# Shifting the weight tiles by 96 bytes and moving the last strip to other PSUM banks in a two-block network kernel

## The chip, the cores and the metric

The kernel runs on one NeuronCore of a Trainium2 chip. The metric is the device time of one execution in microseconds (us). Three timed runs of the kernel before gave 1153.91, 1154.55 and 1156.99 us, so the median is 1154.55 us. The profiled execution, from which all rows below come, took 1154.29 us; its span from the first to the last instruction is 1152.5 us.

## The reference, cut to what matters

The reference is one pass of two transformer-like blocks over 256 tokens of width 1024, in fp32. Nearly all of its arithmetic is matrix products of the 256 token rows with weight matrices that are read once:

```python
# block 1
h = rmsnorm(x, norm_mix);  parts = split(h @ w_in)           # attention, delta rule, gates
x = x + (g0*(ya @ w_oa) + g1*(yb @ w_ob) + g2*(yc @ w_oc)) @ w_out
x = x + memory_cross_attention(...)                          # w_mq, w_mkv, w_mo
x = x + (silu(a) * b) @ w_down                               # a, b from conv(h @ w_up)
# block 2
x = x + 0.5 * rmsnorm(swiglu(h, ffn1_w_gate, ffn1_w_up, ffn1_w_down))
x = x + rmsnorm(concat(moba_attention, pool) @ w_out_2)
x = x + rmsnorm(memory_cross_attention_2(...))               # xa_wq, xa_wkv, xa_wo
x = x + 0.5 * rmsnorm(swiglu(h, ffn2_w_gate, ffn2_w_up, ffn2_w_down))
```

The feed-forward layers have 2816 hidden columns, so that their weights (1024 x 5632 up and 2816 x 1024 down, three times) are more than half of the weight bytes. The attentions are small: 256 tokens and 4 to 8 heads.

## The kernel before, in words

**Products.** TensorE has a fast form for fp32 operands, called fp32r in the kernel, which rounds them. To keep fp32 precision every weight and every activation is held as a rounded part (hi) and the rest (lo), and three products are added: hi times hi, hi activation times lo weight, lo activation times hi weight. `split_weight` makes the parts of a weight piece: ScalarE writes the hi part `wh` from the loaded piece `raw`, VectorE writes the lo part `wl` as `raw - wh`. A piece is 128 partitions by 1024 elements (512 KB) and comes by one DMA from the SP queue. There are 3 `raw` tiles, 4 `wh` and 4 `wl`, in rings.

**Jobs.** A `Job` is one strip of an output: a run of pieces over the contraction. Kind "a" has the weights stationary (128 columns loaded into the array) and an activation part of 256 tokens moving; kind "b" has the activation stationary and 512 columns of the weight part moving. `products` issues a piece's matmuls. A job's sums lie in PSUM banks: `pmm` (3 banks) for jobs, `pat` (5 banks) for the attention chains, norms and transposes. A job of 512 columns of kind "b" takes two banks, one for each half of the tokens.

**Order.** The whole order of instructions is written out by a planner in Python while the kernel is built. `Pace` keeps an estimate of when each engine is free and each value due; `Stream.pick` takes the first piece of a window of at most 4 split pieces that can start, and `Stream.start_of` says whether it can: the activation must be there, and if the job is not begun, its banks plus those of all jobs in `begun` and `pending` must fit into `PMM` = 3, or 2 for a piece that is not first in the window. `Kern.room`, `drop` and `take` do the like for the attention chains with lists of due times (`live`, with 5 entries for `pat`). The planner works with tile names and offsets inside a tile, never with addresses in SBUF.

**The last layer.** `result` makes the end: two jobs of kind "b" on `ffn2_w_down_2`, of 512 output columns each. The second carries `last=True`, which sets `Job.held`: its last two pieces are kept back and then issued bank by bank (`last_pieces`), so that the first half of the tokens can be finished while the second is still summed. When the first strip is done its callback `cb` loads a table into ScalarE, squares both banks on ScalarE (`square`) and multiplies both by a gain on VectorE (`gained`). The last strip is finished by `end`, which also writes the output by DMA.

**SBUF.** Pools lie one behind the other in the order in which `build` opens them, each tile rounded up to 32 bytes in a partition. Adding up the sizes, and taking the start of the activation tiles (`a4`, `g`) as 64 modulo 256, gives: the scratch tiles `s2`, `s1` also 64, the tile of ones `onesr` 128, the weight tiles `wh`, `wl` and `raw` 32. All slices that matmuls of jobs take begin at multiples of 512 bytes inside these tiles.

Of the kernel before, what the change touches and what calls it, by code (L numbers as in the profile page):

```python
# [6 lines left out]
F32 = mybir.dt.float32  # L7
# [4 lines left out]
PSUM = bass.MemoryType.PSUM  # L12

P = 128
# [8 lines left out]
WEIGHTS = 4  # L23
RAWS = 3
PMM = 3
LIMIT = {"s2": 6, "pat": 5, "s1": 3, "row": 4}


# [2 lines left out]
SLACK = 0.15  # L31
# [108 lines left out]
class Pace:  # L140
    HOP = 0.13

    def __init__(self, nc):
        self.free = {"pe": 0.0, "act": 0.0, "dve": 0.0, "pool": 0.0, "dma": 0.0}
        self.due = {}
        self.used = {}
        self.base = {}
        self.rings = {}
        self.count = 0
        self.now = 0.0  # L150
        self.cold = 2
        self.idles = []
        self.tile_before = None
        self.last = 0.0
        self.tensor = Queue(self, nc.tensor, "pe")
        self.scalar = Queue(self, nc.scalar, "act")
        self.vector = Queue(self, nc.vector, "dve")
        self.gpsimd = Queue(self, nc.gpsimd, "pool")
        self.sync = Queue(self, nc.sync, "dma")
# [138 lines left out]
class Act:  # L298


    def __init__(self, K, nk, tag):
        n4 = (nk + 3) // 4
        self.his = [K.a4(F32R, tag) for _ in range(n4)]
        self.los = [K.a4(F32R, tag) for _ in range(n4)]
        self.has_hi, self.has_lo = set(), set()
# [47 lines left out]
class Stream:  # L353
# [3 lines left out]

    def __init__(self, K):
        self.K = K
        self.pace = K.nc  # L360
        self.threads = []
# [83 lines left out]
    def start_of(self, pc):  # L445

        job = pc["job"]
        act = job.act.v
        ks = range(*pc["k"])
        if act is None or not all(k in act.has_hi for k in ks):  # L450
            return None
        if job not in self.begun:
            live = sum(len(j.ps) for j in self.begun + self.pending)
            if live + job.banks > PMM - (pc is not self.window[0]):
                return None
        return max([self.pace.ready(pc["hl"][0])] +
                   [self.pace.ready(act.hi(k)) - 0.2 * (k - ks[0]) for k in ks])
# [41 lines left out]
    def products(self, pc):  # L499


        K, job = self.K, pc["job"]
        nt = job.ncols // P if job.kind == "a" else 2
        if job.held is not None and job.left <= 2:
            job.held.append(pc)
            if len(job.held) == 2:
                self.last_pieces(job.held)
            job.left -= job.left == 2
            return
        if job.kind == "a":  # L510
            at = lambda n: job.ps[n // 2][:, n % 2, :]
        else:
            at = lambda n: job.ps[n].rearrange("p a b -> p (a b)")
        if job.ps is None:
            job.ps = [K.pmm() for _ in range(job.banks)]
            self.begun.append(job)
            first = True
        else:
            first = False
        act = job.act.v  # L520
        hi, lo = pc["hl"]
        ks = range(*pc["k"])
        known = all(k in act.has_lo for k in ks)
        early = known and max(self.pace.ready(act.lo(k)) for k in ks) <= self.pace.now + 0.8
        order = (0, 2, 1) if early else (0, 1, 2)
        for i in order:
            if i == 2:
                self.wait(lambda: all(k in act.has_lo for k in ks))
            for k in ks:
                for n in range(nt):  # L530
                    out = at(n)
                    x = act.lo(k) if i == 2 else act.hi(k)
                    if job.kind == "a":
                        s = (k - ks[0]) * job.ncols + n * P
                        a, b = (lo if i == 1 else hi)[:, s:s + P], x
                    else:
                        s = slice((k - ks[0]) * 512, (k - ks[0]) * 512 + 512)
                        a, b = x[:, n * P:n * P + P], (lo if i == 1 else hi)[:, s]
                    K.mm(out, a, b, first and k == ks[0] and i == 0 and (n % 2 == 0 or job.kind == "b"),
                         job.left == 1 and k == ks[-1] and i == order[-1])  # L540
            if i != order[-1]:
                self.step()
        job.left -= 1
        if job.left == 0:
            self.begun.remove(job)
            self.pending.append(job)
# [13 lines left out]
class Kern:  # L560
    def __init__(self, tc, pools, aps):
# [4 lines left out]
        self.n = 0  # L566
        self.live = {k: [0.0] * m for k, m in LIMIT.items()}

# [51 lines left out]
    def s1(self, tag="s1"):  # L620
        t = self.take(tag)
        w = 16 + T if tag == "row" else T
        return self.nc.begin(self.p["s1"].tile([P, w], F32, tag=tag, bufs=LIMIT[tag], name=self.nm(tag)), t)

# [1417 lines left out]
def build(tc, aps):  # L2042
    from contextlib import ExitStack
    nc = tc.nc
    with ExitStack() as es:
        pool = lambda name, bufs, **kw: es.enter_context(tc.tile_pool(name=name, bufs=bufs, **kw))
        bufs = {"x": 1, "c": 1, "a": 12, "s2": 6, "s1": 3, "tiny": 8, "sq": 4, "rb": 4, "wh": 4, "wl": 4, "raw": 3,
                "pmm": 3, "pat": 5}
        pools = {n: (pool(n, b, **({"space": PSUM} if n in ("pmm", "pat") else {})), b) for n, b in bufs.items()}
        K = Kern(tc, pools, aps)  # L2050
        c = K.p["c"]
        K.onesr = c.tile([P, P], F32R, name="onesr")
        K.vec0 = c.tile([P, NVEC0], F32, name="vec0")
        K.vec = c.tile([P, NVEC - NVEC0], F32, name="vec")
        K.con = c.tile([P, NCON], F32, name="con")
        K.poolw = c.tile([P, 4, P], F32, name="poolw")
        K.ypad = c.tile([P, 4, 260], F32, name="ypad")
        K.cf = c.tile([P, T], F32R, name="cf")
        K.cg = c.tile([P, T], F32R, name="cg")
        K.selr = c.tile([P, 8], F32R, name="selr")  # L2060
        with tc.manual_schedule():
            nc.gpsimd.memset(K.onesr.bitcast(F32), 1.0)
            nc.gpsimd.memset(K.ypad[:, :, 0:4], 0.0)
            nc.gpsimd.memset(K.cf.bitcast(F32), 0.0)
            nc.gpsimd.memset(K.cg.bitcast(F32), 0.0)
            model(K, aps)
# [104 lines left out]
```

## Time and profile before

| | |
|---|---|
| median of three timed runs | 1154.55 us |
| profiled execution | 1154.29 us |
| its span | 1152.5 us |
| PE busy | 1126.1 us (98% of the span), 9108 matmuls |
| PEld (weight loads) busy | 1074.6 us |
| DVE (VectorE) busy | 762.5 us |
| ACT (ScalarE) busy | 668.1 us |
| POOL (GpSimd) busy | 250.1 us |
| mean granted TensorE clock | 0.994 |
| DMA | 193.96 MB, mean 168 GB/s |

Matmuls overlap: one row of the trace says when a group of matmuls began, and the end of a group is modelled. The distance from the beginning of one group to the beginning of the next, divided by the number of matmuls, is therefore the spacing, and it is less than the duration that the profile prints for one matmul. Starts are printed to 0.01 us.

### The profile page before, as it was taken

What the parts mean: (1) busy time and instruction counts of PE and PEld (TensorE: products, weight loads), DVE (VectorE), ACT (ScalarE), POOL (GpSimd) and SP (SyncE); (2) the same over time, 40 slices, a digit from 0 to 9 for tenths busy, and PEclk for the clock granted to TensorE, in tenths of its full rate; (3) what the DMA queues carried; (4) which work ended last, traced back from release to release, by engine and by line L of the source; (5) the groups of instructions that cost most, each with busy time, mean ns of one, the idle gap of its engine ahead of it and who ended that gap; (6) DMA issues with size and microseconds to landing.
All of it is one profiled execution on the core that took longest, in us unless ns stands there. A gap on an engine that the chain in (4) does not pass through costs nothing.

```text
span 1152.5 us, 22341 instructions
## 1 busy us (share of the span) xinstructions
PE 1126.1 (98%) x9108; PEld 1074.6 (93%) x9108; DVE 762.5 (66%) x1015; ACT 668.1 (58%) x1085; POOL 250.1 (22%) x235
## 2 busy tenths in 40 slices
PE   8999999999999999999999999999999998999997
PEld 7998998999988999999999999999989998999976
DVE  6885785558886588998556555448876747555543
ACT  5447773465786566666545554546667557555442
POOL 0020130022141023333015333012102112533200
PEclk9999999999999999999999999999999999999999
DMA  7554533236564365556656555665444534666652
GB/s 244 180 170 152 193 111 111 93 111 199 169 200 146 101 193 183 183 183 190 203 160 218 191 190 177 201 194 160 167 148 147 152 92 140 205 192 207 196 191 91
DMA packets 56550, 193.96 MB, mean 168 GB/s; under 512 B 6400, under 2 KB 6528, under 8 KB 56448
## 3 DMA queue, kind: packets, MB, share of 16 engines
q1 hardware_dynamic: 56304, 192.54, 52.3%
q8 instruction: 71, 1.16, 0.4%
q14 instruction: 31, 0.25, 0.1%
q10 hardware_dynamic: 144, 0.01, 0.0%
HBM read 191.47 MB, written 1.05 MB: 167 GB/s over the span
## 4 chain that ended last, share of the span: by engine, by line
PE 65%; DVE 16%; ACT 7%; issue 6%; DMA 4%; POOL 1%; SPq 0%; DVEq 0%; ACTq 0%; POOLq 0%
PE pmm L291 58%; PE pat L291 8%; DVE wl L291 6%; ACT wh L291 3%; DVE s L291 3%; DVE a L291 3%; DMA raw<-w_in 3%; ACT s L291 2%; DVE g L291 1%; DMA raw<-w_up 1%; DVE sg L291 1%; DVE ypad L291 1%; POOL s L291 1%; ACT g L291 1%; ACT L291 1%
## 5 line engine op out<-in xcount | busy, mean ns | idle before, releaser
L291 DVE TENSOR_TENSOR wl<-raw,wh 128x1024 fp32r<-128x1024 f32 (+1 forms) x370 | 455.3, 1238 | 283.1 <-ACT wh L291 279.4
L291 PE MATMUL pmm<-a,wh 128*128 128x256 f32 x3856 | 505.0, 281 | 7.2 <-DVE a L291 5.2
L291 PEld LDWEIGHTS pmm<-a,wh 128*128 128x128 f32 x3856 | 474.3, 189 | 13.3 <-DVE a L291 6.9
L291 ACT ACTIVATE wh<-raw 128x1024 fp32r<-128x1024 f32 (+1 forms) x370 | 372.5, 1019 | 166.4 <-PE pmm L291 58.1
L291 PE MATMUL pmm<-a,wl 128*128 128x256 f32 x1928 | 269.8, 281 | 2.4 <-DVE wl L291 1.8
L291 PEld LDWEIGHTS pmm<-a,wl 128*128 128x128 f32 x1928 | 244.0, 188 | 5.8 <-DVE wl L291 4.4
L291 PE MATMUL pmm<-g,wh 128*128 128x256 f32 x1088 | 140.3, 280 | 0.1
L291 PEld LDWEIGHTS pmm<-g,wh 128*128 128x128 f32 x1088 | 132.6, 188 | 0.8 <-POOL g L291 0.3
L291 POOL TENSOR_TENSOR sq<-sq,sq 128x512 f32<-128x512 f32 x30 | 41.9, 1398 | 342.4 <-ACT sq L291 304.9
L291 POOL TENSOR_TENSOR s<-s 128x256 f32<-128x256 f32 x66 | 71.9, 1089 | 175.7 <-ACT s L291 169.3
L291 ACT ACTIVATE s<-s 128x256 f32<-128x256 f32 (+4 forms) x118 | 56.1, 478 | 91.2 <-DVE s L291 76.9
L291 POOL TENSOR_TENSOR g<-s,g 128x256 fp32r<-128x256 f32 x66 | 64.5, 978 | 60.0 <-ACT g L291 60.0
L291 PE MATMUL pmm<-g,wl 128*128 128x256 f32 x544 | 75.6, 280 | 0.0
L291 PEld LDWEIGHTS pmm<-g,wl 128*128 128x128 f32 x544 | 68.7, 188 | 0.1
L291 ACT ACTIVATE g<-s 128x256 fp32r<-128x256 f32 x66 | 27.3, 413 | 56.7 <-POOL s L291 56.7
L291 PE MATMUL pmm<-wh,g 128*128 128x512 f32 x208 | 55.4, 405 | 2.9 <-DVE a L291 1.9
L291 POOL TENSOR_TENSOR s<-s,s 128x512 fp32r<-128x512 f32 (+1 forms) x25 | 33.4, 1342 | 105.7 <-ACT s L291 101.0
L291 PEld LDWEIGHTS pmm<-wh,g 128*128 128x128 f32 x208 | 39.8, 193 | 13.0 <-DVE a L291 2.2
L291 DVE SCALAR_TENSOR_TENSOR s<-ypad,vec,s 128x256 f32<-128x256 f32 x88 | 45.7, 578 | 0.0
L291 PE MATMUL pmm<-wh,a 128*128 128x512 f32 x160 | 42.0, 401 | 0.0
L291 DVE TENSOR_TENSOR s<-pmm,rb 128x512 f32<-128x512 f32 x44 | 30.2, 688 | 16.1 <-PE pmm L291 16.1
L291 ACT ACTIVATE a<-x,vec 128x256 fp32r<-128x256 f32 x54 | 24.8, 501 | 21.5 <-DVE x L291 21.4
(165 smaller groups left out, 874.5 us busy)
## 6 DMA issues: line engine op xcount, KB each, us to landing
raw<-ffn_w_up SPq DMA_DIRECT2D x82, 512.0 KB, 4.2
raw<-w_in SPq DMA_DIRECT2D x78, 512.0 KB, 4.3
raw<-ffn_w_down SPq DMA_DIRECT2D x42, 512.0 KB, 4.3
raw<-w_up SPq DMA_DIRECT2D x41, 512.0 KB, 4.3
raw<-w_down SPq DMA_DIRECT2D x20, 512.0 KB, 4.3
raw<-w_out SPq DMA_DIRECT2D x16, 512.0 KB, 4.4
raw<-xa_wkv SPq DMA_DIRECT2D x16, 512.0 KB, 4.0
raw<-w_mkv SPq DMA_DIRECT2D x8, 512.0 KB, 4.1
```

The lines of the kernel that those rows point to most:

```text
L291: return fn(*args, **kwargs)
```

## The change

Two things change. In `build` a pool named `gap` with one tile of 24 fp32 elements (96 bytes in a partition) is opened just ahead of the pool `wh`; nothing reads or writes it. The pools `wh`, `wl` and `raw` behind it start 96 bytes later: `wh` and `wl` go from 32 to 128 modulo 256, where the activations stay at 64. For kind "a" the stationary operand was 32 bytes ahead of (below) the moving one modulo 256, and is 64 bytes behind (above) it.

Second, the job with `held` (the last strip) takes its two banks from `pat` and not from `pmm`: `products` calls `K.pat()` twice, and `start_of` asks for two `pat` banks that are due, and no longer counts the job among the users of `pmm`.

```diff
+GAP = 24
@@ start_of
-            live = sum(len(j.ps) for j in self.begun + self.pending)
-            if live + job.banks > PMM - (pc is not self.window[0]):
+            live = sum(len(j.ps) for j in self.begun + self.pending if j.held is None)
+            if job.held is not None:
+                if len(self.K.live["pat"]) < job.banks or sorted(self.K.live["pat"])[job.banks - 1] > self.pace.now + SLACK:
+                    return None
+            elif live + job.banks > PMM - (pc is not self.window[0]):
                 return None
@@ products
-            job.ps = [K.pmm() for _ in range(job.banks)]
+            if job.held is None:
+                job.ps = [K.pmm() for _ in range(job.banks)]
+            else:
+                job.ps = [K.pat().rearrange("p (a b) -> p a b", a=2) for _ in range(job.banks)]
@@ build
-        pools = {n: (pool(n, b, **({"space": PSUM} if n in ("pmm", "pat") else {})), b) for n, b in bufs.items()}
+        pools = {}
+        for n, b in bufs.items():
+            if n == "wh":
+                pools["gap"] = (pool("gap", 1), 1)
+            pools[n] = (pool(n, b, **({"space": PSUM} if n in ("pmm", "pat") else {})), b)
         K = Kern(tc, pools, aps)
+        K.p["gap"].tile([P, GAP], F32, name="gap")
```

## Rows read from the trace of the kernel before

**Rows 1.** The page: PE's busy time and share, and the granted clock by slices.
```profile
PE 1126.1 (98%) x9108; PEld 1074.6 (93%) x9108; DVE 762.5 (66%) x1015; ACT 668.1 (58%) x1085; POOL 250.1 (22%) x235
PEclk9999999999999999999999999999999999999999
```

**Rows 2.** PE's groups by shape: out<-in, count, busy us, mean ns, idle before.
```profile
L291 PE MATMUL pmm<-a,wh 128*128 128x256 f32 x3856 | 505.0, 281 | 7.2 <-DVE a L291 5.2 <-ACT wh L291 1.7
...
L291 PE MATMUL pmm<-g,wh 128*128 128x256 f32 x1088 | 140.3, 280 | 0.1
...
L291 PE MATMUL pmm<-wh,g 128*128 128x512 f32 x208 | 55.4, 405 | 2.9 <-DVE a L291 1.9 <-DVE sg L291 1.0
L291 PE MATMUL pmm<-wh,a 128*128 128x512 f32 x160 | 42.0, 401 | 0.0
```

**Rows 3.** PE's waits: us in total, times, longest us.
```profile
PE pmm L291 <- DVE wl L291: 1.8, 3, 0.8
...
PE pmm L291 <- ACT wh L291: 1.7, 5, 0.7
```

**Rows 4.** Timeline of PE in a feed-forward layer: start us, us, instruction, count.
```profile
649.97 2.03 PE L291 MATMUL pmm<-a,wh 128*128 128x256 f32 x16
651.84 1.10 PE L291 MATMUL pmm<-a,wl 128*128 128x256 f32 x8
652.77 0.40 PE L291 MATMUL pmm<-a,wh 128*128 128x256 f32 x2
```

**Rows 5.** Timeline of PE: fp32r matmuls of 256 columns with onesr stationary.
```profile
347.58 0.63 PE L291 MATMUL pat<-s,onesr 128*128 128x256 f32 x4
348.06 0.50 PE L291 MATMUL pat<-onesr,s 128*128 128x1 f32 x4
```

**Rows 6.** Timeline of PE: fp32r matmuls of 512 columns with onesr stationary.
```profile
113.82 0.63 PE L291 MATMUL pat<-s,onesr 128*128 128x512 f32 x2
114.29 0.64 PE L291 MATMUL pmm<-a,wh 128*128 128x256 f32 x4
```

**Rows 7.** Timeline of PE: plain fp32 passes of 256 columns, and fp32r behind them.
```profile
366.18 3.61 PE L291 MATMUL pat<-g,a 128*128 128x256 f32 x16
369.44 1.29 PE L291 MATMUL pmm<-a,wl 128*128 128x256 f32 x8
370.56 0.63 PE L291 MATMUL pmm<-a,wh 128*128 128x256 f32 x4
```

**Rows 8.** Timeline of all engines at the end of the last strip.
```profile
1142.99 1.10 PE L291 MATMUL pmm<-wh,g 128*128 128x512 f32 x4
1143.66 0.60 ACT L291 ACTIVATE sq<-pmm 128x512 f32<-128x512 f32 x1 [8.27 <-PE pmm L291]
...
1145.79 0.63 PE L291 MATMUL pmm<-wh,g 128*128 128x512 f32 x2
1146.46 0.60 ACT L291 ACTIVATE sq<-pmm 128x512 f32<-128x512 f32 x1 [1.55 <-PE pmm L291]
```

**Rows 9.** Timeline of all engines where the last strip begins.
```profile
1110.62 1.06 ACT L291 ACTIVATE wh<-raw 128x1024 fp32r<-128x1024 f32 x1 [1.74 <-PE pmm L291]
...
1111.36 2.03 PE L291 MATMUL pmm<-wh,g 128*128 128x512 f32 x8
...
1113.22 1.09 PE L291 MATMUL pmm<-wl,g 128*128 128x512 f32 x4
...
1114.16 0.39 PE L291 MATMUL pmm<-wh,g 128*128 128x512 f32 x1
...
1114.84 1.29 DVE L291 TENSOR_TENSOR sg<-pmm,a 128x512 f32<-128x512 f32 x2 [1.90 <-ACT sq L291]
...
1115.28 1.06 ACT L291 ACTIVATE wh<-raw 128x1024 fp32r<-128x1024 f32 x1
1115.59 1.90 PE L291 MATMUL pmm<-wh,g 128*128 128x512 f32 x7 [1.04 <-DVE sg L291]
```

## The prediction

> **What bounds the kernel now.** [...] The groups by shape say which matmuls [rows 2]: of kind "a" 3856 + 1088 = 4944 with `wh`, and half as many with `wl`, because hi·hi and lo·hi use `wh` and only hi·lo uses `wl`; that is 7416 of 256 columns. Of kind "b" it is 368 and 184, so 552 of 512 columns. Then the timeline gives the spacing, from start to start: in a feed-forward layer 24 matmuls take from 649.97 to 652.77, 2.80 us, so 116.7 ns each [rows 4]; in the last layer 12 matmuls of 512 columns take from 1111.36 to 1114.16, 233.3 ns each [rows 9]. 7416 x 0.1167 = 865 us and 552 x 0.2333 = 129 us: 994 of the 1152.5 us are these two streams, the rest being attention matmuls and gaps between stages. Waits for the weights' parts are small: PE stood 1.8 us for `wl` and 1.7 us for `wh` in the whole run [rows 3].
>
> Is there something in 116.7 ns that an address could give back? Sixteen passes of plain fp32 with 256 columns and the eight fp32r matmuls behind them take from 366.18 to 370.56; less 8 x 0.1167, 3.45 us are left, 215 ns a pass [rows 7]. If fp32r streamed at just twice that rate, 256 columns would take 108 ns and 512 columns 215. So 9 ns of each kind "a" matmul and 18 ns of each kind "b" one are an excess over the doubled plain rate: 7416 x 9 = 67 us and 552 x 18 = 10 us. 77 us is all that a placement of operands could be worth.
>
> **The last strip's banks.** The first strip ends, the last one's first matmul starts at 1114.16 into the third bank, and the next starts at 1115.59, released by VectorE's product on the first strip's bank [rows 9]. Without a wait it would follow after 0.23 us. 1.43 - 0.23 = 1.20 us go when the banks come from `pat`, which has five and serves only chains and norms, none of which runs in the last layer. Everything behind is one stream of matmuls until the last bank is read, so the end moves by the same 1.20 us, if no wait takes its place. What is late next: ScalarE does the first strip's table load and squares between two splits of weights, so `wh` is written at 1115.28 where the step of 2.8 us from 1110.62 would have put it at 1113.42, 1.9 us late [rows 9]. That piece goes into a ring of four whose next use is three pieces of 2.8 us after its slot came free, 8.4 us; the two parts take 1.06 us and some 1.2 us and there are over 5 us of reserve, so 1.9 + 1.2 us fit. No job but this one is planned otherwise, since `held` is None for all the rest and the order of pieces in the window stays. Price: -1.20 us; at worst 0 (the wait comes back as one for `wh`).
>
> **The gap.** It adds no instruction and no wait, and the planner knows no addresses, so the order of all instructions stays. It can only act through where operands lie. For ScalarE, VectorE and the DMA the three tiles `raw`, `wh`, `wl` move together. If a split got slower or faster, the PE would see it only through the 3.5 us of waits above [rows 3]; I take 0, bounds -3.5 and a few us.
>
> For TensorE the question is whether the load of the next weights, which runs beside each matmul, slows the moving stream, and whether that hangs on the distance of the two addresses modulo 256. The trace has the new distance already: `onesr` (128) stationary against `s2` tiles (64) moving is 64 bytes behind, what `wh` against `a` will be. Four such matmuls of 256 columns take from 347.58 to 348.06, 120 ns each, which in starts printed to 0.01 us is 117 to 123 [rows 5]; two of 512 columns take from 113.82 to 114.29, 235 ns each [rows 6]. Against 116.7 and 233.3 at the present distances (-32 for "a", +32 for "b") that is no gain, and a loss of at most 3.3 and 1.7 ns.
>
> A second test needs no address: a matmul beside which no weights load. The last strip ends bank by bank. In its first bank the final two matmuls begin at 1142.99, with the other bank's loads running beside the last of them, and ScalarE, which waits for that bank, starts at 1143.66; in its second bank they begin at 1145.79, nothing loads any more, and ScalarE starts at 1146.46 [rows 8]. Both times 0.67 us. Had the load cost the stream its 18 ns, the second would be one or two hundredths shorter. At the resolution of a hundredth the load is not what makes the 18 ns, and then no distance can bring them back.
>
> Bounds from both sides: -77 us if the whole excess goes [rows 2, 7]; above, 7416 x 3.3 ns + 552 x 1.7 ns = +25.4 us if the new distance costs what the `onesr` rows show at their most [rows 5, 6]. The two rows nearest in kind (same distance, and no load at all) both say that the spacing stays, so I take 0.
>
> [...]
>
> Sum against the profiled execution: 1154.29 - 1.20 + 0 = 1153.1 us. Its time lies 0.26 us under the median of 1154.55, so the two need no correction.
>
> **The rivals.** *The two reads do meet, and the new distance parts them.* For it: the spacing is the same 116.7 ns throughout the dense stretch, an excess which the plain fp32 passes, at half the rate, don't have. Against it: [rows 6, 8]. If a third of the excess goes, 1153.1 - 26 = 1127 us; all of it, 1076 us. A tenth, 1145.4, would be seen already.
>
> *The new distance costs.* The place is the moving stream of every kind "a" matmul, the price at the most the 3.3 ns of [rows 5]: 1153.1 + 25.4 = 1178.5 us, at half of it 1166 us. It decides from (1.2 + 3.5) us / 7416 = 0.6 ns a matmul on, which no row here can exclude. Against it: those four matmuls also change operands and bank at either end, and the 512 column pair shows just 1.7 ns.
>
> *The change doesn't do what it says at the end.* PE waits at the last strip for the late `wh` instead, and the time stays at 1154.3 us.
>
> **How the numbers follow.** The forecast, banks alone, has 0.45, and its own range is 1150 to 1156 us. The empty third rival has 0.05. The parted reads get 0.34, since 77 us of excess has a cause that I can't name from the trace, and I put two thirds of that on gains under 28 us. The cost gets 0.16, three quarters of it below half its price. Within 0.3% (3.5 us, about what a measurement of this kernel can tell from no change): 0.45 + 0.05 = 0.50; faster 0.34; slower 0.16. The range reaches down to a third of the excess, 1125, and up to half of the cost, 1166, and leaves out 0.11 and 0.04.
>
> **What would show it.** The dense stretch of the first feed-forward layer of block 2 shows 24 matmuls in 2.80 us again if the gap does nothing; 2.59 us would be the whole excess, 2.88 us the cost. The last layer's 12 matmuls show 2.80 us likewise. The last strip's second matmul follows its first after 0.23 us, and the wait for `sg` is gone from PE's waits. I am wrong if the spacing anywhere in the dense stretches moves by over 0.6 ns, or if PE waits for `wh` or `wl` in the eight microseconds after the last strip begins.

## The result and the profile after

The changed kernel takes 1143.04 us (median; 1141.01 to 1146.95) beside 1155.28 us for the kernel before: ratio 0.9897, 95% interval 0.9867 to 0.9928. The forecast of 1153.1 us was the case "banks alone, gap at nothing"; what came is the rival in which the distance between the two operands gives back a part of the excess. The profiled execution took 1142.6 us with a span of 1140.8 us, 11.7 us less than before. The order of the matmuls is the same, and the helper's line 291 is line 292 now.

The page of after, engine totals and granted clock by slices:

```profile
PE 1108.9 (97%) x9108; PEld 1058.2 (93%) x9108; DVE 762.9 (67%) x1015; ACT 668.5 (59%) x1085; POOL 252.8 (22%) x235
PEclk9899999999999999999999999999999999999999
```

PE is busy for 17.2 us less than in [rows 1] with the same 9108 matmuls, but the time in which it is not busy grew from 1152.5 - 1126.1 = 26.4 us to 31.9 us. So the matmuls became faster, and 5.5 us of that came back as waiting.

PE's groups by shape in after (out<-in, count, busy us, mean ns, idle before), which answer to [rows 2]:

```profile
L292 PE MATMUL pmm<-a,wh 128*128 128x256 f32 x3856 | 496.9, 280 | 10.4 <-DVE a L292 5.4 <-ACT wh L292 4.0 <-DVE s L292 0.7
...
L292 PE MATMUL pmm<-g,wh 128*128 128x256 f32 x1088 | 137.4, 278 | 0.4 <-DVE g L292 0.4
```

The same counts take 496.9 us for 505.0 and 137.4 for 140.3, while the idle time ahead of the first group rose from 7.2 to 10.4 us, with `wh` as a releaser for 4.0 in place of 1.7.

Two stretches of PE's timeline in after (start us, us, instruction, count). The first is the dense stretch that answers to [rows 4], the second lies in the stage of the convolution:

```profile
642.22 1.98 PE L292 MATMUL pmm<-a,wh 128*128 128x256 f32 x16
644.03 1.07 PE L292 MATMUL pmm<-a,wl 128*128 128x256 f32 x8
644.93 1.98 PE L292 MATMUL pmm<-a,wh 128*128 128x256 f32 x16
```

```profile
479.62 2.05 PE L292 MATMUL pmm<-a,wh 128*128 128x256 f32 x16
481.50 1.10 PE L292 MATMUL pmm<-a,wl 128*128 128x256 f32 x8
482.44 2.05 PE L292 MATMUL pmm<-a,wh 128*128 128x256 f32 x16
```

In the first, 24 matmuls take 2.71 us, 113 ns each (116.7 before); in the second 2.82 us, 117.5 ns. From all starts of the trace, these are two fixed spacings, 113.3 and 117.8 ns. In this trace a stretch keeps the one it has until PE next stops or changes its kind of matmul; the longest, 1487 matmuls from 602 us on, stands at 113.3 ns. Some 1200 of the kind "a" matmuls stood at 117.8, most others at 113.3. The kernel before has two spacings as well: of its settled kind "a" matmuls (those behind the first nine of a stretch) about one in eight stood at 117.8 ns, the others at 116.7. So the change moved the lower of two spacings and left the upper one where it was. The mean over the run went from 116.84 to 114.36 ns, and for kind "b" from 233.15 to 229.59.

PE's waits in after (us in total, times, longest us), beside [rows 3]:

```profile
PE pmm L292 <- ACT wh L292: 4.0, 7, 1.4
PE pat L292 <- DVE x L292: 3.1, 3, 1.9
PE pat L292 <- POOL s L292: 3.0, 4, 1.4
PE pmm L292 <- DVE wl L292: 2.9, 6, 1.1
```

The two waits for weight parts grew from 3.5 to 6.9 us. All of PE's waits together went from 18.9 to 25.3 us, although the one for `sg` at the last strip is gone.

The last layer of after on PE, its passage to the last strip (which answers to [rows 9]) and then its end ([rows 8]):

```profile
1101.63 1.99 PE L292 MATMUL pmm<-wh,g 128*128 128x512 f32 x8
1103.46 1.08 PE L292 MATMUL pmm<-wl,g 128*128 128x512 f32 x4
1104.38 1.99 PE L292 MATMUL pat<-wh,g 128*128 128x512 f32 x8
...
1134.13 0.63 PE L292 MATMUL pat<-wh,g 128*128 128x512 f32 x2
1134.79 0.60 ACT L292 ACTIVATE sq<-pat 128x512 f32<-128x512 f32 x1 [1.50 <-PE pat L292]
```

Twelve matmuls of 512 columns take 2.75 us (2.80 before). All eight of the last strip's first piece run without a stop, in `pat` banks.

### The profile page after: what moved, and what is told of

It is laid out like the page before. It is cut to its first block, busy times and chain, and to the rows that moved or that the text cites. A ratio compares the mean times of both kernels' runs of the same rounds, so it can differ in the third digit from the quotient of the medians.

```text
span 1140.8 us, 22341 instructions
## 1 busy us (share of the span) xinstructions
PE 1108.9 (97%) x9108; PEld 1058.2 (93%) x9108; DVE 762.9 (67%) x1015; ACT 668.5 (59%) x1085; POOL 252.8 (22%) x235
## 4 chain that ended last, share of the span: by engine, by line
PE 70%; DVE 12%; ACT 7%; DMA 5%; issue 4%; POOL 1%; SPq 0%; DVEq 0%; ACTq 0%; POOLq 0%
PE pmm L292 60%; PE pat L292 11%; DVE wl L292 6%; ACT wh L292 3%; DVE a L292 2%; DMA raw<-w_in 2%; DVE g L292 1%; ACT s L292 1%; DVE sg L292 1%; DMA raw<-ffn_w_up 1%; ACT L292 1%; DVE s L292 1%; ACT g L292 1%; DVE x L292 1%; DMA raw<-w_ob 1%
## 5 line engine op out<-in xcount | busy, mean ns | idle before, releaser
L292 PE MATMUL pmm<-a,wh 128*128 128x256 f32 x3856 | 496.9, 280 | 10.4 <-DVE a L292 5.4
L292 PEld LDWEIGHTS pmm<-a,wh 128*128 128x128 f32 x3856 | 466.8, 189 | 17.1 <-DVE a L292 7.2
L292 PE MATMUL pmm<-a,wl 128*128 128x256 f32 x1928 | 266.5, 280 | 3.0 <-DVE wl L292 2.9
L292 PEld LDWEIGHTS pmm<-a,wl 128*128 128x128 f32 x1928 | 240.9, 189 | 6.8 <-DVE wl L292 5.3
L292 PE MATMUL pmm<-g,wh 128*128 128x256 f32 x1088 | 137.4, 278 | 0.4 <-DVE g L292 0.4
L292 PEld LDWEIGHTS pmm<-g,wh 128*128 128x128 f32 x1088 | 130.1, 188 | 1.0 <-DVE g L292 0.6
L292 PEld LDWEIGHTS pmm<-wh,a 128*128 128x128 f32 x160 | 29.4, 188 | 6.8 <-DVE g L292 0.7
L292 DVE SCALAR_TENSOR_TENSOR a<-x,vec,a 128x256 fp32r<-128x256 f32 x56 | 32.9, 623 | 2.3 <-ACT a L292 2.3
```

What stands on the lines that cost most here:

```text
L292: return fn(*args, **kwargs)
```

## The experiments

A name like "distance 64" below means: start of the stationary operand minus start of the moving one, in bytes, modulo 256. Kind "a" goes from 224 to 64 by the change, kind "b" from 32 to 192. The streams below vary the distance from 0 to 240 bytes, so that it repeats after 256 bytes was not tested. Each of the streams alone, and each of the two kernels without taps, was executed once.

**Does the spacing hang on the distance at all?** A stream of matmuls alone, 48 to a distance.

```diff
+for d in range(16):                       # distance 16*d bytes
+    for i in range(48):
+        matmul(o, st[:, (i % 8)*128 + 4*d :][:, :128], mv[:, (i % 4)*256 :][:, :256])
+# then 512 columns, then stationary operands of 32 columns, then both starts moved
```

> A kernel of its own that leaves the network out: groups of 48 fp32r matmuls (24 of 512 columns) with nothing on the other engines, the weights' start varied against the moving start. Theory D (what counts is stationary start minus moving start modulo 256): at 224 a 256 column group has 116.7 ns a matmul, at 64 it has 113.3 ns, as in the two kernels; 512 columns at 32 have 233.3 ns and at 192 have 229.2 ns; moving both starts together changes nothing. Theory S (the weights' own start counts): the four groups with the same distance and other starts differ by 3 ns. On the cause: if the load beside makes the excess over 108 ns, loads of 32 columns in place of 128 leave about a quarter of it, so 110 ns or less at every distance; if the stream makes it by itself, they stay at 113 to 117 ns.

PE's timeline of this stream, one row for each distance: 0 and 16 (from 21.96), 64 and 80 (from 44.74), 224 and what follows (from 101.26), and loads of 32 columns at distances 64, 96 and 128 (from 168.50):

```profile
21.96 5.92 PE L37 MATMUL oc<-mv,st 128*128 128x256 f32 x48
27.72 5.85 PE L37 MATMUL od<-mv,st 128*128 128x256 f32 x48
...
44.74 5.61 PE L37 MATMUL og<-mv,st 128*128 128x256 f32 x48
50.18 5.86 PE L37 MATMUL oh<-mv,st 128*128 128x256 f32 x48
...
101.26 5.76 PE L37 MATMUL oa<-mv,st 128*128 128x256 f32 x48
106.86 5.92 PE L37 MATMUL ob<-mv,st 128*128 128x256 f32 x48
...
168.50 5.62 PE L37 MATMUL oe<-mv,st 128*32 128x256 f32 x48
173.95 5.60 PE L37 MATMUL of<-mv,st 128*32 128x256 f32 x48
179.39 5.61 PE L37 MATMUL og<-mv,st 128*32 128x256 f32 x48
```

From start to start: 5.76 us at distance 0 (120.0 ns each), 5.44 us at 64 (113.3), 5.60 us at 224 (116.7). Of sixteen distances 64 and 192 gave 113.3, the rest 116.6 to 120.1. With 512 columns, 192 gave 229 ns and 32 gave 233; distance 0 was fast there, 227. With both starts moved together, 224 stayed at 116.7, but 64 gave 113.3 twice and 117.8 twice. So the distance decides, and at 64 something more does. Loads of 32 columns came down to 113.3 ns at more distances (also at 96 and 128, where loads of 128 columns stood at 118.8 and 118.5) and never lower. So at some distances the load does slow the stream, but a quarter of the load does not bring back what is left at 113.3.

**The gap alone and the strip alone.**

```diff
 gap alone:    + pools["gap"] ahead of "wh", tile [P, 24];  start_of and products as before
 strip alone:  start_of and products as changed;  no pool "gap"
```

> The gap of 96 bytes without the last strip's other banks. If the gap makes the gain, the time is 1.20 us above the full change (ratio to before about 0.991) and the dense stretch shows 24 matmuls in 2.72 us; if the gain came from the order or the banks, the ratio is 1.00.

> The last strip in the chains' banks without the gap. By the prediction 1.20 us go and nothing else: ratio 0.999, the second matmul of the last strip 0.23 us behind the first, dense stretch 24 matmuls in 2.80 us as before.

The gap alone took 1144.65 us, ratio 0.9921 (0.9891 to 0.9952); the strip alone 1155.43 us, 0.9993 (0.9977 to 1.0009). PE's timeline of the gap alone, the dense stretch and a stretch at 551 us:

```profile
551.60 2.05 PE L291 MATMUL pmm<-g,wh 128*128 128x256 f32 x16
553.48 1.10 PE L291 MATMUL pmm<-g,wl 128*128 128x256 f32 x8
554.43 2.05 PE L291 MATMUL pmm<-g,wh 128*128 128x256 f32 x16
...
639.84 1.98 PE L291 MATMUL pmm<-a,wh 128*128 128x256 f32 x16
641.66 1.07 PE L291 MATMUL pmm<-a,wl 128*128 128x256 f32 x8
642.56 1.98 PE L291 MATMUL pmm<-a,wh 128*128 128x256 f32 x16
```

2.72 us for 24 at 640 us, but 2.83 us at 551 us, a stretch that in the profiled run of after was fast. PE's timeline of the strip alone at the passage to the last strip:

```profile
1111.27 2.03 PE L291 MATMUL pmm<-wh,g 128*128 128x512 f32 x8
1113.14 1.09 PE L291 MATMUL pmm<-wl,g 128*128 128x512 f32 x4
1114.07 2.03 PE L291 MATMUL pat<-wh,g 128*128 128x512 f32 x8
```

No stop is left there, 2.80 us for twelve as before, and the span is 1151.1 us, 1.4 us under that of before. Nearly the whole change in time is the gap's; the strip's 1.2 us are below what timing can tell.

**Is it the distance, or the place of the weights?** The gap in front of the activations moves everything behind it, the weights to 128 as in the change, but the distance stays 224.

```diff
-            if n == "wh":
+            if n == "a":
                 pools["gap"] = (pool("gap", 1), 1)
```

> The same 96 bytes, but in front of the activations: weights at 128 modulo 256 as after the change, activations at 160, so that their distance stays 32 bytes ahead as before. Theory D: spacing 116.7 ns in the dense stretch, ratio 1.00. Theory S (weights' own place, or the place of raw and wh for ScalarE, VectorE and DMA): spacing 113.3 ns, ratio 0.99.

1157.17 us, ratio 1.0011 (0.9995 to 1.0027). The mean spacing was 117.11 ns; no stretch stood at 113.3, nearly half of the settled matmuls at 117.8 and the others at 116.7. Moving the weights does not bring the gain; the distance does.

**A distance that should cost.** A gap of 32 bytes puts stationary and moving operands of kind "a" at distance 0.

```diff
-GAP = 24
+GAP = 8        # no change of the last strip's banks
```

> A gap of 32 bytes in place of 96, so that weights and activations start at the same place modulo 256 (distance 0), with the last strip as before. Theory D with the distances measured alone: 120.0 ns a kind a matmul, 7416 x 3.3 ns = 24.5 us more, and 227.4 for kind b, 552 x 5.9 ns = 3.3 us less; about 1.018 of before, slower. If any move away from 32 bytes ahead helped, it would be faster.

1167.54 us, ratio 1.0089 (1.0061 to 1.0118). PE's timeline in the dense stretch:

```profile
646.24 2.08 PE L291 MATMUL pmm<-a,wh 128*128 128x256 f32 x16
648.16 1.12 PE L291 MATMUL pmm<-a,wl 128*128 128x256 f32 x8
649.12 2.08 PE L291 MATMUL pmm<-a,wh 128*128 128x256 f32 x16
```

2.88 us for 24, 120.0 ns as in the stream alone: a theory that knows only the distance has this spacing right. Its price came to half: over the run kind "a" cost 7416 x 2.99 ns = 22.2 us more and kind "b" 552 x 5.25 ns = 2.9 us less, but the span grew by 11.4 us only. PE's waits shrank from 18.9 to 15.5 us. That table counts a wait only from the modelled end of the matmul before, which lies over 100 ns behind the next possible start (a mean of 281 ns is printed for a kind "a" matmul, where the next one starts after 116.7), and so misses part of it. From all starts, kind "a" spacings of 130 ns and more at a granted clock of 1.00 (waits and changes of operand) held 23.1 us above the run's mean in the kernel before, 14.8 here and 29.5 in after. The 8.3 us that went here account for the 7.9 us that are missing from the price. The slower PE waited less here (15.5 us by the table, beside 18.9), as the faster one of after waited more (25.3).

**Where did the gain of the change go?** In the stage of the convolution VectorE has the taps of the convolution to do beside the splits. Both kernels were run without the taps.

```diff
-        for k in (1, 0):
+        for k in ():
```

> The kernel before without the two earlier taps of the convolution in the first feed-forward layer (the output is that of a convolution of one tap), which takes four VectorE instructions of 0.58 us from each of its 22 units. For comparison with e6. If that stage waited on VectorE, it gets shorter; by the trace PE waits only 0.2 us there for split weights, so I expect under 2 us.

> The changed kernel with the same two taps left out. Theory W (what the matmuls gain in the convolution stage comes back as waits for VectorE's and ScalarE's weight splits): with the load off VectorE the stage is shorter than in e5 by what the spacing gives, 1081 matmuls x 2 to 3.4 ns = 2 to 3.7 us, where the full kernels differ by 0.4 us. If the gain is lost elsewhere (the pace itself), the difference stays near 0.4 us.

Busy time between the same two matmuls, the 3201st and the 4301st (to 0.05 us); before and after as they are, then before and after without taps. The columns are the window, its length in us, the busy us (and instructions) of PE, PEld, DVE, ACT and POOL, the granted clock, DMA's share and its GB/s:

```profile
384.71:516.16 131.45, 130.78 (x1103) 129.31 (x1102) 110.01 (x152) 83.67 (x136) 43.25 (x39) 1.00 0.56 174
```
```profile
385.54:516.59 131.05, 129.12 (x1102) 127.46 (x1101) 110.42 (x152) 83.30 (x136) 43.86 (x39) 1.00 0.56 174
```
```profile
386.18:517.49 131.31, 131.31 (x1102) 131.31 (x1101) 82.62 (x84) 87.20 (x143) 54.00 (x42) 1.00 0.57 181
```
```profile
384.04:513.34 129.30, 129.07 (x1103) 128.74 (x1101) 81.33 (x83) 86.47 (x142) 52.50 (x42) 1.00 0.57 183
```

With the taps VectorE is busy for 110 of 131 us; PE's busy time falls by 1.66 us and the stage by 0.40. PE's waits for `wh` and `wl` in it were 0.2 us before and 2.0 us after. Without the taps VectorE is busy for 82 us; PE's busy time falls by 2.24 us and the stage by 2.01.

This pair does not measure the change, though, for its streams stood elsewhere than those with taps. The first kernel without taps ran at 120.0 ns from 411 to 600 us, the second at 117.8 nearly throughout from 409 to 786 us. By all starts the mean spacing in this stage was 117.05 ns before and 115.10 after, and without taps 119.38 and 116.92. At its 119.38 ns the kernel before got only 0.14 us shorter here without its taps. The whole times of the pair, 1156.39 and 1146.80 us, are not compared for the same reason.

What the rows do show is read at like spacing: 117.05 ns with taps took 131.45 us, 116.92 ns without taps 129.30 us. And with taps the stage hardly follows the spacing. Over the eight profiled runs of the network with taps (two of them stand below) the mean in this stage lay between 114.57 and 119.97 ns, worth 5.9 us over its 1098 kind "a" matmuls, but the stage took between 130.43 and 132.32 us, and the two ends of the spacing took 131.38 and 132.32. So it is VectorE's load that holds this stage: the splits come late, and a faster stream runs into them.

**What picks 113.3 or 117.8?** Groups of 24 matmuls, the network left out, each group behind one "divider" matmul of another length.

```diff
+for d in distances:                        # 19 of them
+    for n in (60, 76, 100, 116, 140, 164, 188, 220):
+        matmul(x, st, mv[:, :n]);  24 matmuls at distance d
```

> Groups of 24 fp32r matmuls of 256 columns alone, each distance eight times, each time behind one other matmul of 60 to 220 columns, which sets the group off at another moment. If the distance decides alone (theory D as it stands), the eight groups of one distance agree. If the distance only allows a fast pace and the moment of the start picks it (theory L, a lock), the eight groups of distance 64 are some at 113.3 and some at 117.8 ns, as the changed kernel's stretches are. Period 256: 192 is as slow as 224 (116.7); period 128: 192 has groups at 113.3 like 64. Steps of 4 bytes around 64: with lines or banks of 16 bytes or more, 60 and 68 lie near 64.

At distance 64 the eight groups stood at 113.3, 113.3, 113.3, 117.8, 117.8, 117.8, 113.3, 117.8. At 60 and 68 bytes none came under 117, at 192 all eight were at 117.8, at 224 they lay between 116.4 and 117.8. So among these distances the fast spacing is 64's alone (192 can have it, and had it in the first stream), and there something ahead of a stream picks one of two. Next, 18 lengths at distance 64, eight groups of each:

```diff
-for n in (60, 76, 100, 116, 140, 164, 188, 220)   at 19 distances
+for n in (64, 76, ... 244): eight times n, at distance 64
```

> The network is left out: only groups of 24 fp32r matmuls of 256 columns at distance 64 run, each behind one matmul of n columns; 18 lengths n from 64 to 244, eight groups of each. Theory S: the length of the divider alone sets the lock, so all eight groups of one n are alike, all 113.3 ns or all 117.8, and some n always gives 113.3 (by the run before, n of 60 to 100 and 188 may). Theory H: the lock also hangs on the state that the divider found, so that a length keeps or swaps it: at some lengths the eight groups alternate between 113.3 and 117.8, and no length turns every slow group into a fast one. Theory R: neither, eight groups of one length fall without an order, about as often on 113.3 as on 117.8. Only under S could a divider in front of the dense stretches win back what is left, (114.36 - 113.33) x 7416 = 7.6 us.

PE's timeline behind dividers of 116 columns:

```profile
159.37 0.22 PE L37 MATMUL x<-mv,st 128*128 128x116 f32 x1
159.42 3.05 PE L39 MATMUL oa<-mv,st 128*128 128x256 f32 x24
162.31 0.22 PE L37 MATMUL x<-mv,st 128*128 128x116 f32 x1
162.36 2.95 PE L39 MATMUL oa<-mv,st 128*128 128x256 f32 x24
165.15 0.22 PE L37 MATMUL x<-mv,st 128*128 128x116 f32 x1
```

The two periods are 2.94 and 2.84 us, and so on in turn: slow, fast, slow, fast. The same alternation holds at 128 to 152 and 176 to 200 columns. From 64 to 108 columns, and at 164, 212, 232 and 244, all eight were fast; at 220 they went slow, slow, fast. The order repeats without chance in it, and it hangs on the length and on what the divider found, which contradicts the theory in which the length alone decides. The spacing found is not all of that, though: at 220 columns a slow group is followed once by a slow one and once by a fast one. What short dividers do to a slow group, that run did not show:

```diff
-    (n,) * 8
+    (100, 116, n, 116, n, 220, 220, n)
```

> The network is left out: again only groups of 24 fp32r matmuls of 256 columns at distance 64, each behind one matmul of n columns. In each row of eight groups the lengths are 100, 116, n, 116, n, 220, 220, n, for n from 32 to 512. The run before showed that 116 and 220 columns turn a fast group (113.3 ns) into a slow one (117.8 ns). If the lock hangs on the length and on the state found, as that run says, the second, fourth and sixth group are slow wherever the one before was fast, and the third and fifth show what n does to a slow state. Theory K: short dividers (up to 108 columns) set the fast state whatever they find: third, fifth and eighth group at 113.3 for these n. Theory H: they only keep what they find: third group at 117.8 for short n, and a row whose sum is longer by 24 x 4.4 ns = 0.11 us for each group that stays slow. Under K a divider in front of the long stretches would be worth a trial, at the 0.13 us that it takes there; under H none is.

From 32 to 92 columns a divider turned every slow group fast, and so did 212, 232 and 512; 100 did too, a little later in the group, and 108, 164 and 244, which keep a fast group fast, left a slow one slow. So in the bare stream a short divider seemed to be a cure, and it was tried in the network.

```diff
+    if job.kind == "a":
+        K.since += 1
+        if first and k == ks[0] and i == 0 and n == 0 and K.since > 300:
+            matmul(out[:, 0:64], a, b[:, 0:64], start=True, stop=False);  K.since = 0
     K.mm(out, a, b, ...)
```

> The changed kernel with 22 short matmuls more: at the beginning of a kind a job, when more than 300 kind a matmuls have gone by since the last one, its first matmul is preceded by one with the same operands cut to 64 columns, which the real one overwrites. Theory K (the runs with the network left out: 64 columns always leave the fast state behind them): each stretch that such a matmul opens runs at 113.3 ns until the next wait of PE, also those that ran at 117.8 in one or another of the runs so far (1487 matmuls from 602 us, 465 from 543 us, 911 from 971 us). Cost 22 x 0.13 = 2.9 us. Gain: in the profiled run of the changed kernel 1188 matmuls stood at 117.8, of which some 400 would lie behind such a matmul, 1.8 us; in the run of the gap alone 3.4 us; in the run without taps 13 us. So against the changed kernel -10 to +1 us, the median about 2 us lower, 1141 us, and its runs closer together. Rival: the place of the start inside the network decides otherwise than in the bare stream, the slow stretches stay, and the time is 2.9 us higher, 1146 us.

> The changed kernel as it is, on the same chip as the run with the short matmuls, so that the two can be compared: 1143 us by the first timing, 1141 to 1147 for single runs. If the two states of the stream make its scatter, its runs lie further apart than those of the kernel with the short matmuls, and one or two of its long stretches stand at 117.8 ns in one execution and at 113.3 in another.

The kernel with dividers took 1152.41 us, ratio to before 0.9968 (0.9951 to 0.9984); the changed kernel as it is 1146.93 us beside it, 0.9918 (0.9885 to 0.9950). PE's timeline with dividers, one at 647 and one at 685 us:

```profile
644.55 2.05 PE L292 MATMUL pmm<-a,wh 128*128 128x256 f32 x16
646.43 1.11 PE L292 MATMUL pmm<-a,wl 128*128 128x256 f32 x8
647.37 0.20 PE L549 MATMUL pmm<-a,wh 128*128 128x64 f32 x1
647.40 2.08 PE L292 MATMUL pmm<-a,wh 128*128 128x256 f32 x16
649.32 1.07 PE L292 MATMUL pmm<-a,wl 128*128 128x256 f32 x8
650.23 1.98 PE L292 MATMUL pmm<-a,wh 128*128 128x256 f32 x16
...
684.68 1.07 PE L292 MATMUL pmm<-a,wl 128*128 128x256 f32 x8
685.59 0.19 PE L549 MATMUL pmm<-a,wh 128*128 128x64 f32 x1
685.62 2.13 PE L292 MATMUL pmm<-a,wh 128*128 128x256 f32 x16
687.58 1.10 PE L292 MATMUL pmm<-a,wl 128*128 128x256 f32 x8
688.52 2.05 PE L292 MATMUL pmm<-a,wh 128*128 128x256 f32 x16
```

At 647 us the divider turns a slow stream fast (8 matmuls from 649.32 in 0.91 us); the next, at 685 us, turns the fast one slow (8 from 684.68 in 0.91 us, 8 from 687.58 in 0.94). Of the 22 dividers sixteen stood behind 24 or more settled matmuls without a break. All ten that met a fast stream left it slow; of the six that met a slow one three left it slow and three turned it fast. In the profiled executions (1153.49 us and 1141.31) the mean spacing was 115.87 ns with dividers and 114.48 without. So the theory of the cure is wrong in the network. There the divider shares its stationary operand and its bank with the matmul behind it and lies at distance 64, where in the stream alone it lay at 0; which of these matters was not tried. The rival had the spacing's failure right, but not its size: it expected 1146 us, since it let the slow stretches stay and did not foresee that fast ones would turn slow.

The second run of the changed kernel shows its scatter: single runs lay from 1141.3 to 1153.8 us, where 1147 was expected as the longest, and further apart than the kernel's with dividers (1150.8 to 1158.9), as was expected. By its median the gain is 9.8 us, by that of the first run 12.2. The profiled execution of the second run had 305 matmuls from 280.5 us at 117.8 ns, of which 250 had run at 113.3 in that of the first. Whether such stretches make the scatter is not shown, since the long runs left no trace.

## Why the prediction was right or wrong, step by step

The time of 1143.0 us lies between the 1125 and 1166 of the prediction, but in the share of a rival: the forecast's own range, 1150 to 1156, missed it. That the wide range holds it comes from the rivals' shares and not from the mechanism that was forecast.

*What bounds the kernel.* Right in the main: the two streams of matmuls are 994 of the 1152.5 us, and the time moved when their spacings moved. It did not move by as much, because the stage of the convolution is held by its splits (VectorE busy for 110 of 131 us). And a 9 in the row of the clock [rows 1] stands for 90% or more, not for the whole clock: from 28.8 to 57.6 us of the kernel before the granted clock was 0.94.

*The last strip's banks, -1.20 us.* Right. The wait for `sg` is gone, no wait for the late `wh` took its place, and the strip alone shortened the span by 1.4 us.

*The gap at nothing.* This step failed: "the two rows nearest in kind [...] both say that the spacing stays, so I take 0". The gain is 116.84 - 114.36 = 2.48 ns for each of 7416 kind "a" matmuls, 18.4 us, and 233.15 - 229.59 = 3.56 ns for each of 552 of kind "b", 2.0 us. The line of 0.6 ns, at which I said I would be wrong, is passed fourfold. Both pieces of evidence were too weak for what was put on them:

- [rows 5, 6] are four and two matmuls at a change of operands. The runs show that the spacing belongs to a stream that has settled: behind a stop even fast stretches begin with slower ones (their first nine average 114 to 116 ns). A settled stream at distance 64 has 113.3 or 117.8 ns, and the 120 ns of [rows 5] are neither.
- [rows 8] have a resolution of 10 ns, and the effect on one matmul of 512 columns is 4 ns. The end of after shows 0.66 us where before showed 0.67. The step from "the load does not make the 18 ns" to "no distance can bring them back" was no inference either. The runs agree with the first half only for the floor (a quarter of the load stays at 113.3 ns; at distances 96 and 128 it took 5 ns off), and they contradict the second.

That the place of one operand beside the other counts for this kind of matmul is what the streams alone show: with the same shapes and the same two operand tiles their spacing was 120.0, 116.7 and 113.3 ns at distances 0, 224 and 64.

*The excess of 77 us as the lower bound.* It held, but was far too wide. The spacing never fell under 113.3 ns, at any distance or size of load that was tried, so no placement that was tried came to the 108 ns of the doubled plain rate. 116.7 - 113.3 = 3.4 ns, 25 us in all, was what one could give kind "a", and 7416 x 2.48 ns is three quarters of it. The quarter that is missing is mostly the stretches at 117.8.

*Splits and waits.* I looked only for splits that become slower. What happened is that PE became faster and met the splits as they were. The account of the profiled run: spacings -18.4 and -2.0, last strip -1.2, together -21.6 us. Of this came back 7.4 us as waits of PE (18.9 to 25.3 us, apart from the 1.0 for `sg` that the strip took away), and about 2.1 us because 21 more matmuls of kind "a" had spacings over 200 ns instead of 117. Where the granted clock was 0.50 and not 1.00 (in before from 29.9 to 33.3 us, for one), kind "a" stood at 213 to 214 ns; after has 37 such spacings and before 24 (the mean granted clock was 0.88 from 28.5 to 57 us and 0.98 from 100 to 200 us of after, beside 0.94 and 1.00 in before). The strip alone has as many spacings over 200 ns, so they need not be the gap's work. That makes -12.1 us; the span shows -11.7. The waits' part is shown for the stage of the convolution by the runs with and without taps; for the other stages before 580 us it is read from the table of waits alone.

*The rivals.* "The two reads do meet" came true in its result, a part of the excess given back by the new distance; that it is the two reads which meet is not shown. Of its three prices the smallest, a tenth of the excess with 1145.4 us, was the nearest to 1143.0. "The new distance costs" is not true of the change: its slower spacing, 117.8 ns, occurs at the old distance too, and the 120.0 ns that would have been this rival's price came at distance 0, not at 64.

## What to carry to other kernels

In this kernel, which is bound by long streams of equal matmuls, 2.48 and 3.56 ns of spacing were nearly the whole gain, and they were not to be read from short groups or from two-digit durations: a bare stream of 48 matmuls for each placement showed in one run that a placement can be faster (113.3 ns at 64 beside 116.7 at 224), though not which of its spacings a stream in the kernel will take. Take the gain of a faster stream stage by stage, as the smaller of what the stream gives and what its suppliers have in reserve; here 9.9 of 21.6 us did not arrive, 7.4 of them because PE waited more. And before a stage is compared over two runs, compare the spacings at which they stood. A cure that works in the bare stream is still to be tried in the kernel, with the operands and banks that it has there: here the mean spacing was 115.87 ns with it and 114.48 without.

## What the runs showed of the hardware

- For fp32r matmuls of 256 columns the spacing hung on the distance of stationary and moving operand: in this case's streams alone (m1_offsets, m2_modes) it was 120.0 ns at 0, 116.7 at 224, 113.3 or 117.8 at 64, and never under 117 at 60 and 68 bytes. With 512 columns it was 227 at 0, 233 at 32 and at 64, 229 at 192 (m1_offsets).
- At distance 64 the stream had two spacings, 113.3 and 117.8 ns, and the faster was kept for 1487 matmuls (after, from 602 us). A single matmul between groups led from one to the other in an order that repeats (m3_dividers: behind 116 columns periods of 2.94 and 2.84 us in turn); the spacing found and the matmul's length were not always enough to tell the next one (220 columns: 2.94, 2.95, 2.85 us).
- Distance 224 showed three spacings in the network: 116.7 for most of the kernel before, 117.8 for about an eighth of it and for nearly half of the kernel whose activations moved too, and 120.0 from 411 to 600 us of the kernel before without taps.
- Why these addresses matter is open. A load of a quarter of the columns removed no part of what is left at 113.3 ns, but brought distances 96 and 128 down to it, from 118.8 and 118.5 (m1_offsets).
- A plain fp32 pass of 256 columns took 215 ns [rows 7], an fp32r matmul of 256 columns 116.7 [rows 4]. What fp32r does to its operands no run measured.
